# One buffer for the recurrence's output sums, and a convolution that computes in place in a buffer of its own

## The chip, the cores and the metric

The kernel runs on one core of a Trainium2 chip. The metric is the device time of one execution in microseconds. An engine is a queue that executes in the order written: TensorE (PE, with its weight loads listed as PEld), VectorE (DVE), ScalarE (ACT), GpSimd (POOL), and SyncE (SP), which here only issues transfers.

## The reference

Two layers of a mixer run over 256 context tokens and 512 latent tokens, width 2048. In each layer one input projection feeds four groups of heads, whose outputs go through one output projection. The recurrent group and the convolution group are what this change touches:

```
pl = split_proj(hl @ w_in[l]);  pc = split_proj(hc @ w_in[l])        # latent, context
yl_f, bl_f, _ = rwkv_direction(...)    # 8 heads of 64, forward; the same backward
o_C = (group_norm(y_fwd + flip(y_bwd)) + bonus_fwd + flip(bonus_bwd)) * silu(pl[10])
o_D = pl[11] * conv3(pl[12] * pl[13], conv_w) * silu(pl[14])
out = concat(o_A, o_B, o_C, o_D) @ w_out[l]
```

The second layer is the last one, and needs the outputs of the latent tokens alone.

## The kernel before

Tokens lie along the free dimension, channels on the 128 partitions. A *projection* (`proj`, `mtile`, `mstep`, L293 to L326) makes 128 channels of `h @ w_in`: weights arrive in four loads of 256 KB (`wr`), ACT casts each to a high part, POOL or DVE subtracts for the low part, and PE does 48 matmuls of 512 columns for the latent tokens and, where the context is wanted, 48 of 256 columns (L306). I count in matmuls of 512 columns, so that one of 256 is a half. The sums lie in a pool `mm` of three PSUM banks, and a bank comes free when the projection is copied or used (`evac`, `gate2`).

Each layer begins with the recurrence (`recurrence`, `rwkv_pipe`). Four pairs of heads, each with 3 segments of 256 tokens in 2 directions, make 24 *passes*, numbered 0 to 23 in each layer here; pass 6 is the first of the second pair. In a pass the state of one segment is carried through four chunks (`seg_chain`: L745, L748, L753 on PE, with small copies by DVE and ACT between them), while the matrix inverse of the next segment and the preparation of the one after it run beside it. A pass ends with its outputs (`seg_y`, L775 and L776), which are copied or added to `yacc` (L783, L785). When a pair is done, `rwkv_merge` (L863) normalises `yacc`, adds `bacc` (L884), gates, and stores it with a DMA (L888), beside the next pair's first pass.

The projections for the next pair, and after them those of the convolutions (`conv`, two in the first layer's recurrence, four in the second's), fill PE between the small matmuls. No order is written out by hand: a scheduler places every instruction by priority when the program is built, with buffers handed out in program order within a tag. A tile that shares a tag with an older one waits until the older one's last reader has finished.

The tags that matter are these, one buffer each. `x`: the `bacc` of pairs 0 and 2, and then each convolution's `x`, its first projection copied out (L1096, L1098). `o`: the `yacc` of pairs 0 and 2, and then each convolution's `o`, its running sum (L1106, L1109). `yacc` and `bacc`: those of pairs 1 and 3. A convolution's first three projections (`x`, the factor for `zp` at L1105, and the factor for L1115) need one `mm` bank each in the second layer.

Of the kernel before, what the change touches and what calls it, by code (L numbers as in the profile page):

```python
# [9 lines left out]
F32 = mybir.dt.float32  # L10
# [11 lines left out]
T = NCTX + NLAT  # L22
# [16 lines left out]
PADW = 774  # L39
# [64 lines left out]
class Kernel:  # L104
# [661 lines left out]
    def seg_y(self, s):  # L766
        l, ft, st, seg, want_y = (s[k] for k in ("l", "ft", "st", "seg", "want_y"))
        GM, SV, UV, AR = (s[k] for k in ("GM", "SV", "UV", "AR"))
        nc, rp, ps = self.nc, self.rp, self.ps
        V, A = nc.vector, nc.scalar  # L770
        if want_y:
            yp = ps.tile([128, 4, 2, 64], F32, tag="ps", name=self.nm("yp"))
            two = lambda t: t.rearrange("p a t -> p (a t)")
            for c in range(4):
                nc.tensor.matmul(out=yp[:, c], lhsT=two(UV[:, c]), rhs=GM[:, c, 1], start=True, stop=False)  # L775
                nc.tensor.matmul(out=yp[:, c], lhsT=two(SV[:, c]), rhs=AR[:, c, :, 1, :], start=False, stop=True)  # L776
            if "yacc" not in st:
                st["yacc"] = rp.tile([128, PADW], F32, tag=("o", "yacc")[ft % 2], name=self.nm("yacc"))
            ycol = st["yacc"][:, seg * SEG:(seg + 1) * SEG].rearrange("p (c t) -> p c t", c=4)
            for h in range(2):  # L780
                hs = slice(64 * h, 64 * h + 64)
                if st.get(("y", seg)):
                    V.tensor_tensor(out=ycol[hs], in0=yp[hs, :, h, :], in1=ycol[hs], op=ALU.add)  # L783
                else:
                    A.copy(out=ycol[hs], in_=yp[hs, :, h, :])  # L785
            st["y", seg] = True
# [302 lines left out]
    def conv(self, l, f):  # L1089
        nc, gp = self.nc, self.gp  # L1090
        V, G, A = nc.vector, nc.gpsimd, nc.scalar
        ctx = l < DEPTH - 1
        cs = slice(0 if ctx else NCTX, T)
        segs = ([(0, 0, NCTX, 2)] if ctx else []) + [(1, NCTX, NLAT, 260)]
        cw = self.P(l, "conv").rearrange("p (k f) -> p k f", k=3)
        x = gp.tile([128, T], F32, tag="x", name=self.nm("x"))  # L1096
        p = self.proj(l, 6336 + f * 128, ctx=ctx)
        self.evac(x[:, 0:NCTX], x[:, NCTX:T], p)  # L1098
        zp = gp.tile([128, PADW], F32, tag="stg" if gp is self.rp else "cz", bufs=2, name=self.nm("zp"))
        for c in (0, 258, 772):  # L1100
            G.memset(zp[:, c:c + 2], 0.0)
        p = self.proj(l, 6848 + f * 128, ctx=ctx)
        for i, o0, n, po in segs:
            with self.tc.high_priority():
                V.tensor_tensor(out=zp[:, po:po + n], in0=p[i][:, 0:n], in1=x[:, o0:o0 + n], op=ALU.mult)  # L1105
        o = gp.tile([128, T], F32, tag="o", name=self.nm("o"))  # L1106
        for i, o0, n, po in segs:
            s = slice(o0, o0 + n)
            A.activation(out=o[:, s], in_=zp[:, po:po + n], func=AF.Copy, scale=cw[:, 1, f:f + 1])  # L1109
            for k, d in ((0, -1), (2, 1)):  # L1110
                V.scalar_tensor_tensor(out=o[:, s], in0=zp[:, po + d:po + d + n], scalar=cw[:, k, f:f + 1],
                                       in1=o[:, s], op0=ALU.mult, op1=ALU.add)
        p = self.proj(l, 5824 + f * 128, ctx=ctx)
        for i, o0, n, po in segs:
            V.tensor_tensor(out=o[:, o0:o0 + n], in0=p[i][:, 0:n], in1=o[:, o0:o0 + n], op=ALU.mult)  # L1115
        sg = self.gate2(gp, self.proj(l, 7360 + f * 128, ctx=ctx), "stg" if gp is self.rp else "cz", 2)
        V.scalar_tensor_tensor(out=o[:, cs], in0=o[:, cs], scalar=0.5, in1=sg[:, cs], op0=ALU.mult, op1=ALU.mult)
        nc.sync.dma_start(out=self.od[12 + f][:, cs], in_=o[:, cs])
# [174 lines left out]
```

## Time and profile before

| | |
|---|---|
| three runs | 3751.83, 3750.08, 3751.13 us; median 3751.13 |
| profiled execution | 3740.13 us, of which its span 3738.3 |
| PE busy, share of the span | 3448.6 us, 92% |
| DVE, ACT, POOL busy | 2303.8, 1863.0, 1364.5 us (62%, 50%, 36%) |
| mean granted TensorE clock | 0.959 of full speed |
| first layer's recurrence, passes 0 to 23 | about 254 to 945 us |
| second layer's recurrence, passes 0 to 23 | 2313 to 2966 us |

In the rows below, busy time of an engine is the union of its instructions in a stretch; the granted clock is a share of TensorE's upper level, so that a mean of 0.68 is a mixture of its two levels, 1.0 (2.4 GHz) and 0.5 (1.2 GHz). Passes are cut at the first L745 matmul of each.

### The profile page before, as it was taken

The page shows a single profiled execution, that of the slowest core. Times are in us where ns is not written, and L with a number is a line of the kernel's source. Part 1 is how long each engine was busy: PE and PEld are TensorE (multiplying, and loading weights), DVE is VectorE, ACT ScalarE, POOL GpSimd, SP SyncE. Part 2 cuts the span into 40 slices and gives each one's busy share as a digit, 9 for nine tenths or more (in the row PEclk, how much of TensorE's full clock was granted, in tenths as well). Part 3 has the DMA queues.
Part 4 walks back from the last instruction along what each step waited for, and adds up shares of the span by engine and source line. Part 5 has one row for each costly group of instructions (what it writes and reads, how often), then busy time and mean ns, then how long its engine had stood idle before and what let it go on. Part 6 is the DMA issues. An engine that isn't in the chain of part 4 may idle for free. (4 is left out here: it accounts for less than half of the span.)

```text
span 3738.3 us, 61946 instructions
## 1 busy us (share of the span) xinstructions
PE 3448.6 (92%) x22388; PEld 2811.2 (75%) x22388; DVE 2303.8 (62%) x4659; ACT 1863.0 (50%) x4131; POOL 1364.5 (36%) x1729
## 2 busy tenths in 40 slices
PE   7999999989999999999897899999778999999998
PEld 2477777767877888888676777777566787788798
DVE  5856777777386546463878734767667526643354
ACT  4466666766244344223324435767666524544454
POOL 2244444534222222222444433545334332322343
PEclk9999999989999999999999999999668999999999
DMA  8432222211343313344655433122011244423565
GB/s 306 183 116 65 59 66 67 60 48 38 104 130 96 112 51 95 112 139 134 201 156 184 123 115 89 56 69 60 28 29 46 60 133 132 139 71 85 166 188 179
DMA packets 239747, 400.90 MB, mean 107 GB/s; under 512 B 25936, under 2 KB 95568, under 8 KB 235344
## 3 DMA queue, kind: packets, MB, share of 16 engines
q1 hardware_dynamic: 232528, 386.45, 34.3%
q10 hardware_dynamic: 6912, 10.49, 0.8%
q8 instruction: 176, 2.88, 0.3%
q14 instruction: 131, 1.07, 0.1%
HBM read 363.28 MB, written 33.56 MB: 106 GB/s over the span
## 5 line engine op out<-in xcount | busy, mean ns | idle before, releaser
L306 PE MATMUL p<-h,wh 128*128 128x512 f32 (+3 forms) x8576 | 2160.1, 349 | 34.5 <-ACT y L1160 10.7
L306 PEld LDWEIGHTS p<-h,wh 128*128 128x128 f32 (+1 forms) x8576 | 1415.4, 190 | 236.1 <-ACT h L276 15.8
L306 PE MATMUL p<-h,wl 128*128 128x512 f32 (+2 forms) x4288 | 1344.5, 350 | 46.1 <-DVE wl L277 28.9
L277 POOL TENSOR_TENSOR wl<-wr,wh 128x512 fp32r<-128x512 f32 (+1 forms) x535 | 768.4, 1439 | 1501.7 <-ACT wh L276 1317.8
L276 ACT CAST wh<-wr 128x512 fp32r<-128x512 f32 (+1 forms) x756 | 465.8, 617 | 974.1 <-PE p L306 772.2
L306 PEld LDWEIGHTS p<-h,wl 128*128 128x128 f32 (+1 forms) x4288 | 748.4, 190 | 147.7 <-DVE wl L277 35.8
L222 DVE SCALAR_TENSOR_TENSOR acc<-gw,sil,acc 128x512 f32<-128x512 f32 (+1 forms) x636 | 458.5, 778 | 27.4 <-DMA gw<-in_w_mod 25.1
L277 DVE TENSOR_TENSOR wl<-wr,wh 128x512 fp32r<-128x512 f32 (+1 forms) x221 | 160.9, 728 | 218.6 <-ACT wh L276 216.8
L804 PEld LDWEIGHTS <-ib 128*128 128x128 f16 x2304 | 133.2, 103 | 138.1 <-issue 70.0
L839 ACT CAST ib<-xa 64x256 f16<-64x256 f32 x480 | 176.2, 367 | 18.0 <-PE xa L809 12.2
L829 DVE TENSOR_TENSOR T<-inv,c 128x256 f16<-128x256 f32 x240 | 98.9, 412 | 34.5 <-PE inv L804 31.4
L1001 DVE TENSOR_REDUCE sm<-s 128x1 f32<-128x256 f32 (+1 forms) x144 | 74.8, 538 | 73.5 <-PE s L999 72.3
L741 POOL TENSOR_SCALAR sp<-SV,pcs 64x64 f32<-64x64 f32 x160 | 80.8, 509 | 105.5 <-DVE SV L762 81.0
L652 POOL TENSOR_TENSOR bk<-t_tw,kr 64x256 f32<-64x256 f32 x96 | 92.9, 968 | 36.1 <-DVE kr L636 32.4
L745 PE MATMUL ch<-SV,GM 128*128 128x128 f32 x384 | 89.5, 317 | 17.5 <-DVE SV L762 10.1
L1008 ACT ACTIVATE e<-s,sm 128x256 f32<-128x256 f32 (+1 forms) x144 | 80.9, 569 | 41.6 <-DVE sm L1005 33.3
L706 PE MATMUL g<-AR,BK 128*128 128x256 f32 (+1 forms) x384 | 96.7, 391 | 3.9 <-DVE BK L658 1.9
L748 PE MATMUL ch<-zs,xb 128*128 128x64 f32 x384 | 81.3, 296 | 15.0 <-ACT zs L747 13.6
L748 PEld LDWEIGHTS ch<-zs,xb 128*128 128x128 f32 x384 | 65.7, 204 | 38.5 <-ACT zs L747 32.5
L753 PE MATMUL ch<-UV,BKT 128*128 128x128 f32 x352 | 85.6, 328 | 9.6 <-ACT UV L750 8.6
L762 DVE SCALAR_TENSOR_TENSOR SV<-ch,pcs,sp 64x64 f32<-64x64 f32 x256 | 72.1, 281 | 35.4 <-PE ch L753 28.2
L745 PEld LDWEIGHTS ch<-SV,GM 128*128 128x128 f32 x384 | 64.4, 204 | 37.6 <-issue 9.3
(270 smaller groups left out, 5022.0 us busy)
## 6 DMA issues: line engine op xcount, KB each, us to landing
wr<-in_w_in SPq DMA_DIRECT2D x484, 256.0 KB, 2.7
wr<-in_w_out SPq DMA_DIRECT2D x256, 256.0 KB, 2.9
gw<-in_w_mod SPq DMA_DIRECT2D x192, 256.0 KB, 3.0
gw<-in_w_mod SPq DMA_DIRECT2D x32, 1024.0 KB, 6.6
gw<-in_w_mod SPq DMA_DIRECT2D x128, 128.0 KB, 3.2
raw<-rkvd SPq DMA_DIRECT2D x96, 128.5 KB, 2.2
lz<-lzd SPq DMA_DIRECT2D x48, 256.0 KB, 3.1
os<-od SPq DMA_DIRECT2D x32, 256.0 KB, 3.2
```

Source lines behind the costliest of these rows:

```text
L222: self.nc.vector.scalar_tensor_tensor(out=acc, in0=w, scalar=s, in1=acc, op0=ALU.mult, op1=ALU.add)
L276: self.nc.scalar.copy(out=hi, in_=raw)
L277: eng.tensor_tensor(out=lo, in0=raw, in1=hi, op=ALU.subtract)
L306: nc.tensor.matmul(out=p[0:w, 0:n], lhsT=a[:, kk, :], rhs=x[b][k], start=(first and kk == 0 and i == 0), stop=(last and kk == 3 and i == 2))
L652: G.tensor_tensor(out=bk[hs, :, h, :], in0=c4(an)[hs], in1=kn[hs], op=ALU.mult)
L706: nc.tensor.matmul(out=g[:, c], lhsT=bkc(c2 + c), rhs=AR[:, c2 + c, :, 0:nk, :], start=True, stop=True)
L745: nc.tensor.matmul(out=chp[:, 0:128], lhsT=two(GM[:, c, 0]), rhs=two(SV[:, c]), start=True, stop=True)
L748: nc.tensor.matmul(out=chp[:, 128:192], lhsT=XT32[:, c, :], rhs=zs, start=True, stop=True)
L753: nc.tensor.matmul(out=chp[:, 192:320], lhsT=BKT[:, c, :], rhs=two(UV[:, c]), start=True, stop=True)
L804: nc.tensor.matmul(out=out[:, c, :], lhsT=lhsT[:, c, :], rhs=rhs(c), **kw(c))
L829: V.tensor_tensor(out=T1, in0=p1, in1=bt(self.lm(d, j)), op=ALU.mult)
L839: A.copy(out=half(XT, h), in_=aXT[hs])
```

## The change

`yacc` gets one buffer under its own tag, for all four pairs: no pair's outputs go to `o` any more, and each pair's first copy waits for the store of the pair before. In the recurrence's pool the convolution's `x` moves to the tag `o`, which nothing holds after the preparation of the two decay inputs, and the convolution sums in place: `o` is the same tile as `x`, so `x` is overwritten at L1110 of the new kernel once L1106 has read it. The convolutions of the later phase keep their two tiles.

```
-                st["yacc"] = rp.tile([128, PADW], F32, tag=("o", "yacc")[ft % 2], name=self.nm("yacc"))
+                st["yacc"] = rp.tile([128, PADW], F32, tag="yacc", name=self.nm("yacc"))
...
-        x = gp.tile([128, T], F32, tag="x", name=self.nm("x"))
+        own = gp is self.rp
+        x = gp.tile([128, PADW if own else T], F32, tag="o" if own else "x", name=self.nm("x"))
...
-        o = gp.tile([128, T], F32, tag="o", name=self.nm("o"))
+        o = x if own else gp.tile([128, T], F32, tag="o", name=self.nm("o"))
```

The instructions stay the same but for names; what changes is the order that the scheduler makes. It differs on every engine from the end of pass 6 to the end of the first layer's recurrence, and from pass 8 of the second layer's recurrence to the first projections of the attention behind it; elsewhere it is the same row for row. Three places are shown.

ACT in the second layer, where the first convolution's first projection is copied out (`x`, L333). In the kernel before this stands in pass 18 (`ch_30892` is that pass's third chunk), behind the merge of pair 2 (`yacc_29403`, `gn`), and the running sum `o` right behind it:

```order
L877 ACTIVATE gn_30801<-vp_30803,eps 128x256
L882 ACTIVATE yacc_29403<-yacc_29403,par_82 128x256
L594 ACTIVATE kr_31014<-raw_31015,mu_123 128x4x64
L747 COPY zs_30893<-ch_30892 64x64
L333 COPY x_32220<-p_32221 128x512
L276 CAST hi_30881<-t_L_30779 128x256
L594 ACTIVATE t_zk_31023<-raw_31020,mu_123 128x256
L750 COPY UV_30615<-ch_30892 64x64
L1109 ACTIVATE o_32373<-zp_32295,par_82 128x512
```

In the changed kernel it stands in pass 8 (`ch_27063` is that pass's second chunk), among the inverse (`X`, `ib`, `xa`) of the next segment:

```order
L626 ACTIVATE t_L_27107<-t_L_27107 128x256
L276 CAST hi_27116<-t_sq_27113 128x256
L835 CAST X_27056<-xa_26978 128x256
L839 CAST ib_22698<-xa_26978 64x4x64
L276 CAST wh_32336<-wr_32334 128x512
L333 COPY x_32218<-p_32219 128x512
L839 CAST ib_22698<-xa_26978 64x4x64
L750 COPY UV_26955<-ch_27063 64x64
L632 ACT_TABLE_LOAD
```

The copy moved ten passes forward, ahead of the preparation of pair 2.

PE in the second layer, the last chunk of pass 13 (`ch_29048` before, `ch_29046` now), with the matmuls of the inverse (L848) and of the scores (`g`, L706) around it. Before:

```order
L706 MATMUL g_29093<-AR_22696,BK_29024 128x256 x2
L848 MATMUL inv_29067<-X_5371_29065,GM_28784 128x128
L748 MATMUL ch_29048<-zs_29049,xb_22704 128x64
L848 MATMUL inv_29067<-X_5371_29065,GM_28784 128x128 x3
L706 MATMUL g_29098<-AR_22696,BK_29024 128x256
L753 MATMUL ch_29048<-UV_28802,BKT_28446 128x128
L706 MATMUL g_29098<-AR_22696,BK_29024 128x256
L713 MATMUL bt_29103<-cst,BK_29024 128x128 x4
L745 MATMUL ch_29117<-SV_28781,GM_28784 128x128
```

Now:

```order
L306 MATMUL p_32756<-h_21042,wh_32777 128x512
L745 MATMUL ch_29046<-SV_28440,GM_28443 128x128
L306 MATMUL p_32756<-h_21043,wh_32777 128x512
L306 MATMUL p_32756<-h_21042,wl_32778 128x512
L848 MATMUL inv_29065<-X_5369_29063,GM_28782 128x128
L748 MATMUL ch_29046<-zs_29047,xb_22702 128x64
L848 MATMUL inv_29065<-X_5369_29063,GM_28782 128x128 x3
L706 MATMUL g_29096<-AR_22694,BK_29022 128x256
L753 MATMUL ch_29046<-UV_28800,BKT_28444 128x128
L706 MATMUL g_29096<-AR_22694,BK_29022 128x256
```

Where no projection stood, three matmuls of one (`p_32756`, the last projection of the second convolution) now stand around the chunk's first matmul.

ACT in the first layer, after pass 6, where the outputs of pair 1 are first copied to `yacc_4820`, while the merge still works on `yacc_2344` of pair 0. Before:

```order
L877 ACTIVATE gn_4787<-vp_4789,eps 128x256
L747 COPY zs_4855<-ch_4854 64x64
L785 COPY yacc_4820<-yp_4811 64x256 x2
L695 COPY SV_4828<-vp_4823 64x4x64
L331 COPY stg_5865<-p_5744 128x256
L696 COPY SV_4828<-vp_4823 64x4x64
L882 ACTIVATE yacc_2344<-yacc_2344,par_80 128x256
L750 COPY UV_4849<-ch_4854 64x64
```

Now:

```order
L276 CAST hi_5007<-t_sq_5004 128x256
L742 ACTIVATE sp_4951<-SV_4463,pcs_4324 64x64
L598 COPY zv_4924<-zv_4924 128x4x64
L747 COPY zs_4955<-ch_4954 64x64
L785 COPY yacc_4820<-yp_4811 64x256 x2
L714 COPY BKT_4832<-bt_4843 128x512
L750 COPY UV_4849<-ch_4954 64x64
```

The copy moved behind the second chunk's `zs` (`ch_4954`) of pass 7; the copy `BKT` stood behind it before too, and still does.

## Rows read from the trace of the kernel before

**Rows 1.** Page, 40 slices of the span: tenths of PE busy, and granted clock.

```profile
PE   7999999989999999999897899999778999999998
PEclk9999999989999999999999999999668999999999
```

**Rows 2.** Windows: stretch, length, busy PE PEld DVE ACT POOL (count), clock, DMA, GB/s.

```profile
2313.40:2586.40 273.00, 259.68 (x2186) 205.14 (x2187) 200.93 (x478) 191.86 (x486) 132.53 (x234) 0.99 0.23 65
2586.40:2844.50 258.10, 194.33 (x1476) 156.76 (x1475) 174.21 (x432) 164.48 (x418) 91.03 (x196) 0.68 0.10 28
2844.50:2963.50 119.00, 111.10 (x866) 83.35 (x866) 83.15 (x199) 74.69 (x192) 53.45 (x85) 0.99 0.19 52
2963.50:3071.00 107.50, 107.50 (x482) 88.43 (x481) 26.36 (x35) 35.55 (x57) 39.00 (x37) 1.00 0.39 112
```

**Rows 3.** Windows of line L306 alone (PE, PEld), passes 10 to 18, second layer.

```profile
2586.40:2844.50 258.10, 5.09 (x11) 2.10 (x11) 0.68 0.10 28
```

**Rows 4.** Timeline, pass 18: start, length, engine, line [idle before, releaser].

```profile
2837.95 0.72 POOL L884 TENSOR_TENSOR yacc<-yacc,bacc 128x256 f32<-128x256 f32 x1
...
2838.70 0.59 ACT L333 COPY x<-p 128x512 f32<-128x512 f32 x1 [0.75 <-POOL yacc L884]
...
2841.18 0.72 ACT L1109 ACTIVATE o<-zp,par 128x512 f32<-128x512 f32 x1 [0.23 <-DMA od<-yacc]
```

**Rows 5.** Timeline, ACT, copies of first projections behind the recurrence.

```profile
2984.93 0.58 ACT L333 COPY x<-p 128x512 f32<-128x512 f32 x1
...
3028.45 0.58 ACT L333 COPY x<-p 128x512 f32<-128x512 f32 x1
...
3071.97 0.58 ACT L333 COPY x<-p 128x512 f32<-128x512 f32 x1
```

**Rows 6.** Windows, second layer, passes 6, 8, 9, 12, 13, 21, 22.

```profile
2466.10:2502.70 36.60, 34.49 (x269) 27.49 (x268) 25.36 (x57) 25.31 (x60) 16.18 (x28) 1.00 0.21 62
2530.00:2557.30 27.30, 25.79 (x212) 19.20 (x211) 20.98 (x49) 19.14 (x49) 14.40 (x26) 1.00 0.25 69
2557.30:2586.40 29.10, 27.98 (x224) 21.28 (x223) 21.93 (x52) 22.41 (x54) 17.19 (x28) 1.00 0.26 73
2639.50:2676.50 37.00, 24.78 (x170) 18.96 (x169) 25.60 (x61) 23.14 (x57) 12.43 (x27) 0.63 0.10 30
2676.50:2700.60 24.10, 18.30 (x153) 14.18 (x151) 17.37 (x44) 18.52 (x46) 10.14 (x21) 0.72 0.11 32
2898.50:2930.50 32.00, 29.27 (x229) 22.57 (x230) 22.75 (x52) 21.09 (x51) 15.50 (x24) 1.00 0.14 38
2930.50:2951.40 20.90, 19.96 (x179) 14.85 (x178) 12.55 (x33) 10.76 (x32) 6.08 (x10) 1.00 0.14 40
```

**Rows 7.** Windows, first layer, passes 12, 18, 19.

```profile
610.10:644.60 34.50, 31.98 (x250) 25.25 (x249) 26.04 (x56) 22.72 (x56) 15.52 (x25) 1.00 0.21 60
784.20:818.20 34.00, 24.26 (x173) 17.74 (x171) 24.24 (x55) 19.72 (x50) 11.05 (x22) 0.71 0.07 21
818.20:853.70 35.50, 33.83 (x280) 29.17 (x281) 27.03 (x62) 26.25 (x62) 16.87 (x28) 0.94 0.25 72
```

**Rows 8.** Timeline, first layer: first outputs of pair 1 against pair 0's store.

```profile
471.32 0.75 ACT L785 COPY yacc<-yp 64x256 f32<-64x256 f32 x2 [0.65 <-PE yp L776]
...
475.68 0.32 SPq L888 DMA_DIRECT2D od<-yacc  x1
...
479.58 0.21 ACT L747 COPY zs<-ch 64x64 f32<-64x64 f32 x1
```

**Rows 9.** Page, DMA issues: KB each, median us to landing.

```profile
od<-yacc SPq DMA_DIRECT2D x4, 384.0 KB, 2.5
...
rot<-in_rot SPq DMA_DIRECT2D x2, 64.0 KB, 4.1
```

**Rows 10.** Timeline: last outputs of the second layer, and their merge's store.

```profile
2966.82 0.39 PE L776 MATMUL yp<-AR,SV 128*128 128x128 f32 x2
...
2984.28 0.33 SPq L888 DMA_DIRECT2D od<-yacc  x1
```

## The prediction

> **What bounds the kernel now.** I read the page's slices first: PE is busy nine tenths almost everywhere, and its granted clock is full except in slices 29 to 31 of 40, where busy drops to seven tenths and the clock to 0.6 [rows 1]. That is the second layer's recurrence. The windows cut it by its passes: 0 to 9 last 273.0 us with PE busy 259.7 at a clock of 0.99; 10 to 18 last 258.1 us with PE busy 194.3 at 0.68; then 119.0 us to the end, and 107.5 us of convolution projections with PE busy throughout [rows 2]. In passes 10 to 18 PE runs eleven projection matmuls [rows 3]: the filler is gone. Its cause is in pass 18: the first convolution's `x` is copied out of PSUM at 2838.70, right at the end of the `bacc` addition that last reads the tag `x` (2837.95 + 0.72), and `o` starts at 2841.18, released by the store of `yacc`, which held the tag `o` [rows 4]. Until then the convolution's first three projections fill the three banks of `mm`, and no projection can start.
>
> The price of filler comes from two places. Behind the recurrence the `x` copies of successive convolutions stand 43.52 us apart [rows 5], for 4 projections of 48 matmuls: 0.2267 us a matmul. In the recurrence I counted from the order 249,088 projection columns in passes 0 to 9, that is 486.5 matmuls of 512, or 110.3 us; the other 162.7 us are the passes' own. Pass 6, with a merge, has 74.5 matmuls in 36.6 us [rows 6], own time 19.7; the other nine passes average 15.9.
>
> **The change, part by part.** *Second layer, what leaves.* From the last pass's first chunk to the end of the second attention projection (`k`), the order before has 471 matmuls more than the new one (13 + 9 x 48 of convolution, 26 of `q`). Gone from there: 471 x 0.2267 = 106.8 us, all on the path, since PE is busy 107.5 of 107.5 us there [rows 2].
>
> *What arrives.* Passes 10 to 18 get 488 matmuls instead of 11. If they then behave like the filled ones they last 7 x 15.9 + 2 x 19.7 + 488 x 0.2267 = 261.3 us, against 258.1: 3.2 us lost. This is the centre of the argument: a pass without filler is no shorter than one with it. Pass 12 takes 37.0 us bare and its counterpart, pass 6, takes 36.6 filled; pass 13 is 24.1 bare, while passes 8 and 9, filled with 55 and 54 matmuls of the first convolution, take 27.3 and 29.1 [rows 6]. Passes 19 to 22 get 6 matmuls fewer: 1.4 us gained. Together 106.8 - 3.2 + 1.4 = 105.0 us.
>
> What hides the other work that moves along: the stretch behind the recurrence, with two and a half convolutions and their weight splits, has DVE, ACT and POOL busy 26, 36 and 39 us; added to 174, 164 and 91 in passes 10 to 18 that is 200, 200 and 130 of 258 [rows 2], the share that DVE has in pass 8 already (21.0 of 27.3) [rows 6]. The weight loads go into SP's queue ahead of the recurrence's own loads, and the DMA share rises from 0.10 to the 0.25 of pass 8 [rows 6]. The `zp` memsets on POOL move with them and are too short to count. If this cover fails, a pass is longer by what pass 21 shows: 32.0 us with 50 matmuls is an own time of 20.7, where its kind (pass 9: 29.1 with 54) has 16.9, so +3.8; pass 22, 20.9 with 36, has 12.7, so -3.2 against the average [rows 6]. Passes 19 to 22 together, 2844.5 to 2951.4 [rows 2, 6] with 177 matmuls, average 16.7, 0.8 above; I take 0, and 2 us a pass either way, 26 us over 13 passes, for the range.
>
> *The first layer* has the same stop, once: pass 18 has 13 matmuls in 34.0 us at a clock of 0.71 [rows 7]. The new order puts 79.5 there, 3.5 more in pass 19 and 46 more in the others: 116 that leave the stretch behind, 26.3 us. The 46 cost 10.4. Pass 18 becomes 19.6 of its own (pass 12: 34.5 less 68 x 0.2267 is 19.1; pass 6 by the same reckoning 20.0) plus 18.0, or 37.6: 3.6 lost. Pass 19, 35.5 at a clock of 0.94, becomes 33.9: 1.6 gained. Net 13.9 us.
>
> *The one `yacc`.* Pair 1's first copy ran at 471.32; pair 0's store was issued at 475.68 [rows 8] and lands 2.5 us later [rows 9], at 478.2. At its old place the copy would wait 6.9 us, with ACT's whole queue behind it, the chain's `zs` and `UV` first. At its new place it follows the second chunk's `zs`, which ran at 479.58 [rows 8]; the wait is then gone. What remains is one of two `ps` banks held some 8 us longer. There are three such changes of pair in the first layer; the second layer's first two passes of a pair give no output, so none there. I take 2 us in all; bounds 0 and 3 x 6.9 = 21.
>
> *In place.* A convolution's `x` must now wait for the store of the one before it, 2.5 us by the store of `yacc` [rows 9], but its own projection lies between (10.9 us): nothing. If that cover goes, at most 2.5 us of filler four times.
>
> *The end of the recurrence.* Convolutions used to cover the last merge, from the last outputs at 2966.82 to its store at 2984.28 [rows 10]. Now the rest of `k` does, 61 matmuls or 14 us, and the attention's tables are loaded behind that store on SP: some 17.5 us and 4.1 for `rot` [rows 9], while PE stands at its `rot` matmul after 14 us of `k`, 2 of merge and 4 of `v`. With `x` of the attention in one buffer, `v` waits once more. I take 6 us, bounds 0 and 20.
>
> *Sum.* 105.0 + 13.9 - 2 - 6 = 111 us. The profiled execution took 3740.1, so 3629; the median of the runs is 11.0 above that execution, and from it comes 3640, which I predict.
>
> A filled stretch has PE busy 95% (259.7 of 273.0) and weight loads 75% (205.1) [rows 2]. The Trainium skill, Perfetto Trace Analysis, section Identifying the Most-Contended Engine, calls matmul busy a poor measure for TensorE and takes the share of weight loads; by it a quarter of a filled pass would be free. The 49.5 matmuls a pass would then cost nothing and the sum would be some 14 us better. The trace speaks against it: a pass grows with its filler, 36.6 with 74.5 against 27.3 with 55.
>
> **The rivals.** *The chain and the filler add up (slower).* If each chunk, waiting behind filler in PE's queue, delays the next by all of it, passes 10 to 18 take 258.1 + 477 x 0.2267 = 366 us, both layers' gains vanish, and the 6 us at the end and up to 21 us of `yacc` remain: up to 3751 + 27 = 3778. It decides from a mean of 41 us a pass. For it: the bare passes have PE idle only 25% of the time. Against: passes 8 and 9.
>
> *The clock stays low (slower).* If filled passes kept the 0.68 of the bare ones, 261.3 would become 384 us: 3751 - 106.8 - 1.4 + 126 + 8 - 14 = 3763. Filled passes 8, 9, 21 and 22 all show 1.00 [rows 6], after PE had been busy 95% of its time. The Trainium skill, TensorE: Matmul & The Clock Gate, section A second HAM failure mode: psum-queue depth-cycling, describes a stream that cycles through PSUM banks and oscillates between the levels; by that rule this rival would come true, and those four windows do not bear it out.
>
> *The convolution's own work hurts.* Every one of 13 passes costs the 3.8 us of pass 21: 50 us less gain, 3690. For it: pass 21 itself, and DVE at 78%. Against: pass 22.
>
> *Nothing moves.* `x` finds another wait and the banks stay full: 3751. The order shows the copy ten passes earlier, so this needs a wait that the order doesn't show.
>
> **How the numbers follow.** Forecast 0.83, convolution's work 0.10, chain 0.03, clock 0.02, nothing 0.02. The range is the forecast's with its bounds: 26 us of pass length either way gives 3614 to 3666, the longer waits at the end and of `yacc` (14 and some of 19) stretch the upper end to 3680; I take 3616 to 3680, which leaves half of the second case and the slower ones out. A change of 0.2%, 7.5 us, is what a measurement can tell. Faster are the first two cases, 0.93; same 0.02; slower 0.05.
>
> **What would show it.** Right: passes 10 to 18 of the second layer with about 54 projection matmuls each, a clock of 0.95 or more, and 255 to 280 us in all; hardly 15 us of projections between the last outputs and the attention; pass 18 of the first layer without its idle time; no ACT wait over 2 us before L785. Wrong: a mean over 31 us in those nine passes, L785 waiting for the store with `zs` late behind it, or PE idle for over 15 us at the first attention.

## The result, and the profile after

The changed kernel takes 3644.8 us (median of four runs, 3642.8 to 3646.8), the kernel before 3750.6 (3742.5 to 3751.8). The ratio is 0.9722, with a 95% interval of 0.9705 to 0.9739: 105.8 us faster by the medians, where 111 were predicted. The profiled executions, 3646.3 and 3740.1, are 93.8 us apart; the four runs of the kernel before lie nine microseconds apart, and its profiled execution was shorter than all of them.

The page's slices of the changed kernel (PE busy and granted clock, in tenths) answer to [rows 1].

```profile
PE   6999999999999999999988899999999998999998
PEclk9999999999999999999998999999999999999999
```

The hole in slices 29 to 31 is gone, and with it the clock of 0.6. The windows of the second layer's recurrence answer to [rows 2]; the columns are the same.

```profile
2311.80:2587.40 275.60, 261.21 (x2185) 206.35 (x2186) 203.90 (x481) 193.07 (x488) 133.30 (x234) 0.99 0.22 65
2587.40:2851.30 263.90, 249.15 (x1954) 188.49 (x1953) 200.83 (x456) 189.95 (x462) 132.55 (x234) 0.99 0.24 69
2851.30:2966.00 114.70, 110.27 (x871) 81.60 (x870) 80.05 (x197) 74.11 (x195) 54.74 (x83) 1.00 0.19 54
2966.00:2984.00 18.00, 17.06 (x98) 14.26 (x97) 9.22 (x11) 7.02 (x12) 4.35 (x5) 1.00 0.18 53
```

Passes 10 to 18 are the second row: 263.9 us where they took 258.1, at a clock of 0.99 where it was 0.68. The 107.5 us of projections behind the recurrence have shrunk to part of the last row. What arrived is seen in the groups of line L306 within these nine passes, against eleven matmuls in [rows 3], and in the copies of the four convolutions' first projections, which in [rows 4, 5] began at 2838.70:

```profile
L306 PE MATMUL p<-h,wh 128*128 128x512 f32 x326 | 122.1, 426 | 0.0
L306 PE MATMUL p<-h,wl 128*128 128x512 f32 x162 | 68.8, 425 | 0.0
```

```profile
L333 ACT COPY x<-p x4: 578/583/590, 2539.4 to 2852.8; 128x512 f32<-128x512 f32 x4
```

326 and 162 make the 488 that the order gave. The first `x` is copied at 2539.4, 299 us earlier than before, the fourth at 2852.8, and no idle time stands before any of them: no wait for the in-place buffer is seen.

The first layer, against [rows 7]: the windows of pass 13, pass 18 and pass 19, and then line L785's output copies of pair 2 with what they waited for.

```profile
651.00:688.30 37.30, 33.64 (x277) 27.82 (x276) 25.98 (x57) 24.64 (x59) 15.45 (x27) 1.00 0.25 75
798.20:834.80 36.60, 34.69 (x266) 27.68 (x264) 28.99 (x63) 24.10 (x57) 16.01 (x26) 1.00 0.19 52
834.80:869.10 34.30, 32.79 (x273) 27.08 (x273) 24.79 (x57) 23.50 (x57) 16.05 (x28) 1.00 0.23 66
```

```profile
L785 ACT COPY yacc<-yp x2: 367/368/368, 661.4 to 661.8; 64x256 f32<-64x256 f32 x2
  DMA od<-yacc: 0.2, 1
```

Pass 18 is full. The one wait for the shared `yacc` is 0.2 us, in pass 13; at the other two changes of pair there is none, and VectorE's additions to `yacc` (L783) never wait for it.

The end of the second layer's recurrence, which answers to [rows 10], is where the changed kernel stands. Rows of the timeline of PE, SP, ACT and DVE from 2983, with what the engine waited for in brackets:

```profile
2983.09 0.33 SPq L888 DMA_DIRECT2D od<-yacc  x1
2984.15 0.73 PE L306 MATMUL p<-h,wh 128*128 128x512 f32 x2 [0.84 <-ACT x L333]
2985.38 1.49 SPq L898 DMA_DIRECT2D cs<-in_rope  x1
2986.91 0.43 SPq L900 DMA_DIRECT2D rot<-in_rot  x1
2990.27 0.70 PE L959 MATMUL rot<-x,rot 128*128 128x512 f32 x1 [1.73 <-DMA rot<-in_rot]
2992.86 0.69 DVE L963 TENSOR_TENSOR x<-x,rs 128x512 f32<-128x512 f32 x1 [0.73 <-POOL x L962]
2995.64 0.72 ACT L220 ACTIVATE acc<-gw,sil 128x512 f32<-128x512 f32 x1 [11.54 <-DMA gw<-in_w_mod]
2996.27 1.24 ACT L969 CAST q<-x 64x512 fp32r<-64x512 f32 x2
2998.67 0.37 ACT L331 COPY x<-p 128x256 f32<-128x256 f32 x1 [1.16 <-DVE q L971]
2999.10 0.80 PE L306 MATMUL p<-h,wh 128*128 128x256 f32 x2 [3.58 <-ACT x L331]
```

PE stands three times, 6.2 us in all: for a copy, for the table `rot`, and for `k`'s copy into the one buffer `x`, which `q` holds until ACT and DVE have worked on it. The rotated `q` is ready at 2993.55 (2992.86 + 0.69), but ACT's queue has the scaling of a modulation weight (L220) first, which waits for its load until 2995.64: `q`'s casts begin at 2996.27, 2.7 us late.

### The profile page after: what moved, and what is told of

Its sections match the earlier page's. It is cut to its first block, busy times and chain, and to the rows that moved or that the text cites. A ratio compares the mean times of both kernels' runs of the same rounds, so it can differ in the third digit from the quotient of the medians.

```text
span 3644.5 us, 61929 instructions
## 1 busy us (share of the span) xinstructions
PE 3408.4 (94%) x22388; PEld 2760.2 (76%) x22388; DVE 2314.2 (63%) x4659; ACT 1859.2 (51%) x4131; POOL 1360.0 (37%) x1729
## 5 line engine op out<-in xcount | busy, mean ns | idle before, releaser
L306 PE MATMUL p<-h,wh 128*128 128x512 f32 (+3 forms) x8576 | 2193.8, 352 | 40.4 <-ACT x L331 11.7
L306 PEld LDWEIGHTS p<-h,wh 128*128 128x128 f32 (+1 forms) x8576 | 1420.5, 191 | 240.2 <-ACT h L276 16.2
L306 PE MATMUL p<-h,wl 128*128 128x512 f32 (+2 forms) x4288 | 1356.2, 353 | 40.0 <-DVE wl L277 26.1
L306 PEld LDWEIGHTS p<-h,wl 128*128 128x128 f32 (+1 forms) x4288 | 752.7, 191 | 138.8 <-DVE wl L277 32.2
L804 PEld LDWEIGHTS <-ib 128*128 128x128 f16 x2304 | 118.9, 99 | 124.4 <-issue 67.3
L839 ACT CAST ib<-xa 64x256 f16<-64x256 f32 x480 | 175.9, 367 | 20.0 <-PE xa L809 13.9
L706 PE MATMUL g<-AR,BK 128*128 128x256 f32 (+1 forms) x384 | 92.3, 375 | 3.3 <-DVE BK L658 1.9
L835 ACT CAST X<-xa 128x256 f16<-128x256 f32 x192 | 71.3, 372 | 46.9 <-PE xa L809 44.2
L646 DVE TENSOR_TENSOR AR<-kr,Pt 64x512 f32<-64x512 f32 (+1 forms) x96 | 90.5, 943 | 2.8 <-ACT Pt L621 0.8
L748 PEld LDWEIGHTS ch<-zs,xb 128*128 128x128 f32 x384 | 60.7, 189 | 32.4 <-ACT zs L747 24.8
L634 DVE RECIPROCAL t_sq<-t_sq 128x256 f32<-128x256 f32 x48 | 84.1, 1752 | 1.5
```

Source lines behind the costliest of these rows:

```text
L306: nc.tensor.matmul(out=p[0:w, 0:n], lhsT=a[:, kk, :], rhs=x[b][k], start=(first and kk == 0 and i == 0), stop=(last and kk == 3 and i == 2))
L634: V.reciprocal(out=sq, in_=sq)
L646: V.tensor_tensor(out=AR[hs, :, h, 0:nk, :], in0=kr[hs, :, 0:nk, :], in1=Pva[hs, :, 0:nk, :], op=ALU.mult)
L706: nc.tensor.matmul(out=g[:, c], lhsT=bkc(c2 + c), rhs=AR[:, c2 + c, :, 0:nk, :], start=True, stop=True)
L804: nc.tensor.matmul(out=out[:, c, :], lhsT=lhsT[:, c, :], rhs=rhs(c), **kw(c))
L839: A.copy(out=half(XT, h), in_=aXT[hs])
```

## The experiments

**The layers apart.** In each of two kernels both edits hold in one layer (`LL` is 1 or 0), and the other layer keeps what was there before:

```
-  st["yacc"] = rp.tile(..., tag="yacc", ...)
+  st["yacc"] = rp.tile(..., tag=("o", "yacc")[ft % 2] if l != LL else "yacc", ...)
-  own = gp is self.rp
+  own = gp is self.rp and l == LL
```

The second layer alone:

> Both edits in the second layer alone; the first layer keeps the two buffers for the output sums and the convolution's x and o of before. Theory (the whole gain is second-layer filler; in the profiled pair the matching instructions of the second layer moved by 92 us): 3750.6 - 92 = 3658, passes 10 to 18 of the second layer in 255 to 270 us with a clock over 0.95. Theory on the first layer, kept: its 9 us of the profiled pair are a true gain that a chance of the output phase hid, so this kernel is 9 us above the changed one, 3654. Theory on the first layer, given back: the output phase behind it takes back what the recurrence gains, whatever the run, so this kernel is within 2 us of the changed one, 3645 to 3647.

Measured: 3653.2 against 3741.8 us, 88.6 faster, ratio 0.9757 (0.9743 to 0.9772).

The first layer alone:

> Both edits in the first layer alone; the second layer is as before. First layer kept: 3750.6 - 9 = 3742, and passes 10 to 18 of the second layer bare, 258 us at a clock of 0.6 to 0.7. First layer given back: 3749 to 3751, first attention 9 us earlier, the start of the second layer within 2 us of before. Prediction as made: 13.9 - 2, that is 3739. Waits of the output copies for the one buffer: 0.2 us in all by the changed kernel's profile, up to 21 by the prediction's bound.

Measured: 3726.1 against 3741.8, 15.6 faster, ratio 0.9956 (0.9941 to 0.9971). The windows of passes 10 to 18 of the second layer, of the kernel with that layer changed:

```profile
2599.90:2862.20 262.30, 247.73 (x1953) 187.30 (x1952) 200.30 (x456) 189.83 (x462) 132.17 (x234) 1.00 0.24 70
```

and of the kernel with the first layer changed:

```profile
2575.60:2831.30 255.70, 191.07 (x1477) 153.84 (x1476) 174.18 (x433) 164.36 (x418) 91.16 (x196) 0.69 0.10 29
```

The parts add up: 88.6 + 15.6 = 104.2. The first layer's gain is kept: in the profile of the kernel with that layer alone the first attention begins 11.5 us earlier than before and the second layer still 10.0. It seemed lost in the first pair of profiles, where the first attention began 8.1 us earlier and the second layer only 1.6. Between the two lies a stretch (first attention to the second layer's recurrence) whose order is one and the same in the kernel before, the changed kernel and the seven others here that keep the one buffer of the attention's `x`. In their ten profiles it takes 1286.2 to 1296.5 us: 1290.0 before, 1286.2 to 1295.4 in the seven whose second layer has the convolution as before, 1295.2 to 1296.5 in the three where it has the new buffers. So a few microseconds there say nothing of the first layer. Whether the new buffers cost some 4 us there, or the three were long by chance, stays open.

**One buffer, convolution as before.** Only the tag of the output sums is changed:

```
-  tag=("o", "yacc")[ft % 2]
+  tag="yacc"
```

> One buffer for the output sums of all head pairs, but the convolution as before (x in the tag x, o in the tag o). Theory (each convolution needs both tags free; x still waits for the bacc of pair 2): no gain, 3747 to 3755; the second layer's passes 10 to 18 stay bare, and in the first layer the stop moves one pass ahead (pass 17 half empty, 18 bare), 0 to 4 us lost. Rival (the tag o, held by the output sums, was the stop that counted): passes 10 to 18 of the second layer fill, and over 50 us are gained, 3700 or less. Rival (the one buffer is dear): 3765 to 3772, the copies of the output sums waiting 7 us at each of three changes of pair.

Measured: 3756.6 against 3741.8, 14.9 slower, ratio 1.0040 (1.0026 to 1.0055). The theory had a loss of 0 to 4 us. The last rival had the size, 14 to 21 us, but not the cause: the copies wait 0.2 us for the one buffer in this profile too. The second layer's passes 10 to 18 stayed bare, as the theory said; the loss is in the first layer, whose attention starts 15 us late. Passes 17 and 18 are left with 25 and no matmuls there, as the theory also had it, but passes 7 to 15 take more of the convolution (39 matmuls by the order) and 277.0 us in place of 264.7. The windows of line L306 alone in passes 16 to 18 (length, busy PE, PEld, clock, DMA; the count is of matmuls of either width), here:

```profile
745.10:832.60 87.50, 19.56 (x66) 10.75 (x66) 0.81 0.11 31
```

in the kernel before:

```profile
732.70:818.20 85.50, 32.46 (x117) 18.47 (x117) 0.89 0.14 38
```

and in the kernel with the first layer changed:

```profile
744.50:831.40 86.90, 52.43 (x217) 33.77 (x217) 1.00 0.19 55
```

With 66, 117 and 217 matmuls (58.5, 96.5 and 163 of 512 columns) the three passes take 87.5, 85.5 and 86.9 us, at clocks of 0.81, 0.89 and 1.00. Filler taken out of a pass gives no time back, while passes 7 to 15, which are full already, are 12 us longer with 39 matmuls more: this is the prediction's centre, seen from its other side.

**Filler that does nothing.** Why is a bare pass no shorter? Four kernels add dummy matmuls, whose results nothing reads, to passes 10 to 18 of the second layer of the kernel before. The first three write unused columns of the chain's own PSUM tile, in the first two like this, with ten or four of them:

```
+  fill = lambda: [nc.tensor.matmul(out=chp[:, 320:512], lhsT=self.eyef,
+                                   rhs=self.c16[:, 0, 0:3, :], start=True, stop=True)
+                  for _ in range(10 if l == 1 and 10 <= s["n"] <= 18 else 0)]
   nc.tensor.matmul(out=chp[:, 0:128], ...)
+  fill()
```

and so behind the chain's other two matmuls of a chunk. With ten:

> The kernel before, with 30 matmuls of 192 fp16 columns that nothing reads added to each chunk of the chain in passes 10 to 18 of the second layer, ten behind each of its three matmuls (1080 in all, 0.08 us of columns each at the full clock, 86 us of PE in all). They feed no buffer and need none. Theory (the bare pass is bound by the round trips of the chain through DVE and ACT, and filler lies in their gaps while the clock rises): the nine passes still take 250 to 270 us, the clock 0.9 or more, the time within 10 us of before. Rival, clock (a bare pass is long only because its own matmuls run at 0.68): the nine passes drop by the 44 us that their own 194 us of PE are above the 150 us that filled passes need, to 215 to 225, the time to about 3710. Rival, sum (filler is added to the chain): 86 us or more longer, 3837.

Measured: 3778.9 against 3741.8, 37.1 slower, ratio 1.0093 (1.0078 to 1.0108). With four in place of ten:

> The kernel before with 12 dummy matmuls to each chunk of passes 10 to 18 of the second layer, four behind each matmul of the chain in place of ten (432 in all; by the 0.107 us that one took, 46 us of PE). The ten cost 36 us in nine passes for 116 us of PE. Theory (a block of ten holds PE 1.07 us, longer than the chain's copy takes, so each chunk waits for the end of it; short pieces of filler fit in the gaps): 255 to 263 us for the nine passes, at a clock above that of before (0.68). Rival, share (31% of filler is always paid): 258 + 14 = 272. Rival, clock: with the clock back and little filler, the passes become shorter than bare ones, under 250.

Measured: 3766.3 in one run. With ten, at low priority:

> The same 1080 dummy matmuls as in the kernel with ten behind each chain matmul (36 us longer in the nine passes), but emitted at low priority, so that the scheduler puts them where it sees PE without other work: 39 blocks of ten are left where there were 76, and 36 single ones where there were 3; most are in pieces of one to nine. Theory, place (a piece of filler costs what it holds up behind it; the convolution's projections, placed by the scheduler one or two at a time, cost 6 us for 111): 262 to 280 us for passes 10 to 18 in place of 294, the clock 0.9 or more, the time 3745 to 3763 by the medians of before. Rival, dose (a fixed share of PE work is paid, whatever its place): 290 to 298 us, 3778. Rival, the convolution's projections are hidden because they need no wait on ch: this kernel no better than the other, 294 or more.

Measured: 3814.9 against 3745.8, 69.0 slower, ratio 1.0188 (1.0158 to 1.0217). The nine passes of the three, in this order, each from its own profile:

```profile
2588.20:2882.10 293.90, 235.87 (x2520) 204.70 (x2519) 178.02 (x433) 161.50 (x415) 90.12 (x197) 0.97 0.09 26
```

```profile
2591.10:2870.30 279.20, 225.89 (x1895) 185.07 (x1894) 175.79 (x430) 163.77 (x418) 91.03 (x196) 0.76 0.09 26
```

```profile
2593.60:2925.20 331.60, 255.07 (x2581) 209.75 (x2580) 185.47 (x444) 172.19 (x431) 95.65 (x201) 0.94 0.08 23
```

All my expectations of length were wrong, but for the third rival of the last one, and the design was at fault. The groups of DVE show its copy of `UV` in the nine passes and what it waited for, in the kernel before and in the first of these:

```profile
L749 DVE COPY UV<-ch 64x64 f32<-64x64 f32 x36 | 7.5, 209 | 10.5 <-PE ch L748 10.3
...
L754 DVE COPY UV<-ch 64x64 f32<-64x64 f32 x36 | 7.8, 216 | 31.9 <-PE ch L738 30.7 <-ACT gn L880 0.9
```

L738 is the dummies' line in the second row, L748 the chain's own matmul in the first. The copy reads columns that the dummies don't touch, but they write the same tile, and it waits for their end, 30.7 us where it had waited 10.3 for the chain. DVE's other readers of the tile wait for L738 too, in all three kernels. The dummies were a part of the chain, and these kernels measure a longer chain, not filler. The fourth kernel gives them a bank of `mm` that nothing else uses:

```
+  if s["n"] == 10 and n == 0:
+      self.fill = self.mm.tile([128, 512], F32, tag="mm", ...)
+  with self.tc.high_priority(offset=-1000):
+      for _ in range(13):
+          nc.tensor.matmul(out=self.fill, lhsT=self.eyef, rhs=self.c16[:, 0, 0:8, :], ...)
```

> The kernel before with 468 dummy matmuls of 512 fp16 columns (as long as a projection matmul), at low priority, into a bank of mm that nothing else uses or reads in the second layer's passes 10 to 18; in the two kernels with dummies in the chain's own tile ch, the profile showed DVE's copies waiting for the dummies, so that these lay on the chain. Here nothing waits for them, and they bring no work for DVE, ACT or the queues. By the order 362 come to stand in passes 10 to 17, 104 in passes 5 to 9 in place of 115 matmuls of the convolution, which has two banks in place of three; 64 convolution matmuls more come behind the recurrence, 14.5 us. Theory (filler that nothing waits for lies in the gaps of PE): passes 10 to 17 take 218 to 232 us (221.3 bare, 225.8 in the changed kernel), the clock there 0.9 or more, the time 3746 + 15 = 3755 to 3770. Rival, share (a third of any filler is paid, as with the dummies of ch): 221 + 27 = 248. Rival, sum: 221 + 82 = 303. Rival, clock (bare passes are long only because of 0.68; with the clock back and no other work they are shorter): under 212.

Measured: 3733.8 against 3743.4, ratio 0.9968 (0.9956 to 0.9981): 468 matmuls that compute nothing make the kernel before faster, though 64 of the convolution's are left over at the end. Passes 10 to 17 in its profile, whole, and the dummies' line alone:

```profile
2580.10:2783.40 203.30, 194.04 (x1664) 127.32 (x1663) 149.52 (x372) 141.86 (x363) 78.92 (x174) 0.99 0.11 33
...
2580.10:2783.40 203.30, 102.16 (x362) 31.35 (x362) 0.99 0.11 33
```

the same eight passes of the kernel before:

```profile
2586.40:2807.70 221.30, 169.84 (x1308) 137.88 (x1307) 147.97 (x372) 140.53 (x360) 78.71 (x171) 0.67 0.10 28
```

and of the changed kernel, whole and line L306 alone:

```profile
2587.40:2813.10 225.70, 214.02 (x1706) 161.97 (x1705) 173.53 (x394) 163.31 (x399) 113.66 (x201) 0.99 0.24 69
...
2587.40:2813.10 225.70, 130.96 (x408) 69.92 (x408) 0.99 0.24 69
```

This is the case that I had called the clock's rival: 203.3 us, under its 212. DVE no longer waits for a dummy anywhere. Successive dummies start 0.21 to 0.23 us apart, so the 362 hold PE for some 79 us, and the eight passes are 18 us shorter than bare ones: 97 us in all.

The rows say where these 97 us come from, by estimate. PE's time without work falls from 51.5 us (221.3 less 169.8) to 9.3 (203.3 less 194.0): 42 us of the dummies lie in gaps. Its busy time rises by 24 us for 79 us of dummies: its own matmuls take 55 us less, some 115 in place of 170, as the granted clock goes from 0.67 to 0.99. In the changed kernel the gaps fall to 11.7 us, and 408 matmuls at 0.2267 us are 92.5 of the 214.0, so that PE's own work takes some 122: 40 us of gaps and 48 us of clock stand against 92.5 us of filler. So the theory of the gaps and the rival of the clock are each about half of it: a bare pass has gaps that filler can use, and it runs PE's own matmuls slowly for want of filler. What a bare pass would take at the full clock was not measured, so how much of the gaps would go by the clock alone stays open.

**The end of the recurrence.** The changed kernel again, as the base:

> The changed kernel once more, unaltered, as the base for the two that build on it and to see whether its first layer's gain is given back. Kept (the first-layer kernel kept its 13 us to the end): in this profile the first attention starts 8 to 12 us earlier than in the profile of before, and the second layer's recurrence 5 to 15 us earlier, the output phase between the layers varying by 5 us or more from run to run at one and the same order. Given back: it starts within 3 us of before, as in the first profile.

Measured: 3641.6 against 3744.4, ratio 0.9717 (0.9696 to 0.9738). The first attention starts 8.9 us earlier than in the profile of before, as "kept" had it, the second layer's recurrence 3.3 earlier, short of its 5 to 15; the stretch between, with its spread, is the one described above. Then two buffers for the attention's `x`, and what shares its tag:

```
-  x = tT("x")
+  x = tT("x", 2)
```

> The changed kernel with two buffers for the attention's x (and what shares its tag), so that k can be copied out of PSUM before q is worked up. Theory (the end of the recurrence was priced at 6 us and cost some 12 because k's copy waits for q's, which waits for the tables): PE's 3.6 us without work at 2999 in the changed kernel's profile go, and the like waits of four later attentions (2.4, 1.5, 2.4, 2.1, 3.0 us) go in part: 3 to 12 us faster than the changed kernel. Rival (the banks fill again one projection later, and v waits instead; what bounds the entrance is q's work on DVE and ACT): within 2 us of it, PE without work for the same time in the next place.

Measured: 3629.1 against 3744.4, ratio 0.9686 (0.9667 to 0.9705), 12.5 us below the base by the medians: the theory's gain, a little above its range. PE's list of waits between 1000 and 3500 us (what waited, for what: us in all, times, longest) has in the changed kernel

```profile
PE p L306 <- DVE wl L277: 21.7, 14, 3.7
...
PE p L306 <- ACT x L331: 11.7, 5, 3.6
...
PE s L997 <- ACT e L1008: 4.7, 1, 4.7
...
PE tp L942 <- ACT x L331: 4.3, 4, 2.1
```

and with two buffers

```profile
PE p L306 <- DVE wl L277: 29.6, 19, 4.0
...
PE s L997 <- ACT e L1008: 7.8, 5, 3.1
...
PE tp L942 <- ACT x L331: 0.6, 1, 0.6
```

Of 16.0 us for the copies into `x`, 0.6 are left, and 11.0 come back as waits for weight splits and exponentials. From the start of the second layer's last pass to the first `rot` matmul of its second attention (L959) this kernel takes 120.7 us; the changed kernel took 124.9 and 125.5 in its two profiles, the kernel with the second layer alone 122.8. So 2 to 5 us at the end of the recurrence hung on the one buffer. More lies elsewhere: the second layer's recurrence already starts 7.3 us earlier than in the profile of the base. With the table `rot` loaded first and the first modulation job an attention later:

```
+  self.rot = ...; nc.sync.dma_start(out=self.rot, ...)    # ahead of self.cs
-  mod_jobs(1)
+  if h or l == 0:
+      mod_jobs(1)
```

> The kernel with two buffers for x, and besides: the small table rot loaded ahead of cs, and in the second layer the first job on the modulation weights (whose first scaling on ACT waits 2.1 us for its load, with q's copies queued behind it) started one attention later. Theory: PE's 1.7 us at its rot matmul go down to under 0.5, and q's copies follow at once: 3 to 6 us faster than the kernel with two buffers alone, 6 to 15 faster than the changed one. Rival (the table cs bounds, which DVE needs right behind rot, and it lands no earlier): within 2 us of the kernel with two buffers.

Measured: 3627.3, ratio 0.9685 (0.9666 to 0.9705): no different from two buffers alone, so the rival holds. PE still waits 1.3 us for `rot`, after 1.4. DVE's first use of `cs` (L962 here) is released by the landing of `cs`, 37.8 us behind the start of the last pass, after 38.5:

```profile
2983.58 0.69 DVE L962 TENSOR_TENSOR rs<-rot,cs 128x512 f32<-128x512 f32 x1 [7.37 <-DMA cs<-in_rope]
```

`q`'s casts follow it at once, so the scaling is out of their way and nothing is gained by it. What that scaling costs with one buffer, where `k`'s copy stands behind `q`'s, was not run.

## Why the prediction was right, and where it was off

*The middle of it* was right. The order's 488 matmuls came, and the nine passes took 263.9 us (262.3 with that layer alone) for a predicted 261.3, at 0.99. "The chain and the filler add up" (366 us), "the clock stays low" (384) and "nothing moves" are refuted; "the convolution's own work hurts", which had 3.8 us more a pass, found 2.6 us more in all nine. The section of the Trainium skill on which the clock's rival leaned (TensorE: Matmul & The Clock Gate, section A second HAM failure mode: psum-queue depth-cycling) ties its oscillation to short idle times of PE between groups of matmuls; a stretch that goes through three banks with PE busy 94% stays at 0.99 here. That a pass without filler is no shorter was read from the rows rightly, but without its cause. The dummies show it, by the estimate above: PE's gaps, and the clock, each worth about half of the filler. One of the readings was weak: that "a pass grows with its filler, 36.6 with 74.5 against 27.3 with 55", for the first of the two passes has a merge, 3.8 us of own time by the prediction's own count.

*The term that was mis-sized is the end of the recurrence*, taken at 6 us. Against 106.8 us of matmuls that left, the second layer behind the start of its last pass gained 95.1 (the profiles' gain of 93.8 at the end, and 1.3 lost at that pass): the term is 11.7, inside its bounds (9.9 and 12.9 by two other profiles with the same order there). All of it is lost in the first two attentions: at the third one's first `rot` matmul the gain is 94.3 already. The waits above are 6.2 of it; the kernel before has none there. The granted clock of 0.93 at 2984 to 3010, where PE is busy 20.5 us, is 1.4 more by estimate, and in the 30 us behind that PE is busy 24.95 where the kernel before had 27.30, another 2.4; 1.7 are not placed. I had counted the table's landing, and one more turn of the one buffer at `v`. What I missed is that `k`'s copy stands behind `q`'s whole work-up, 3.6 us of waiting for PE; two buffers take that wait away and give 2 to 5 us back. That the modulation weight's scaling in ACT's queue makes up to 2.7 of the 3.6 is read from the timeline, not shown by a run.

*The first layer*, 13.9 less 2, is 15.6 by the runs (11 to 22) and 11.5 at the first attention by the profile. The kernel with that layer alone shows its parts: 26.3 us leave, as the order had it (its last pass starts 14.8 us later than before, its first attention 11.5 earlier); the passes lose 16.5 where I had 12.4, and 7.2 of that in pass 13 (38.2 against 31.0), for 12 more matmuls by the order, 2.7 us. The kernel with the one buffer alone has that long pass too (37.3), the one with the second layer alone hasn't (31.0); whether the buffer or the order that comes with it makes it was not told apart. Waits for the one buffer, 2 us with a bound of 21, were 0.2.

*Smaller terms.* Passes 19 to 22 gained 5.5 us for a predicted 1.4 (106.9 to 101.4), and passes 0 to 9, left out of the sum, lost 2.6 (273.0 to 275.6). No wait for the in-place buffer was seen. The share of weight loads, by which (beside the share of peak arithmetic) the Trainium skill, Perfetto Trace Analysis, section Identifying the Most-Contended Engine, judges TensorE, would have put the sum 14 us better, away from what was measured; in the filled passes PE's busy time (94%), not that of its weight loads (188.5 of 263.9 us), is nearly full. The 49.5 matmuls a pass of that paragraph are 48.7 by its own count (486.5 in ten passes); nothing else rests on them.

*The base, and luck.* The 11 us between profile and median were not a constant of the kernel: its median was 3741.8 to 3750.6 in five measurements. The gain by medians, 103 to 106 us, is what the sum of 111 must be held against: 5 to 8 us too much. That 3640 came so near to 3644.8 and 3641.6 is in part luck, since from a base of 3742 the same sum gives 3631. And the sum is nearer than its parts: by layers it was 99.0 and 11.9, the runs gave 88.6 (85 to 96) and 15.6 (11 to 22). The second layer was over-forecast by some 10 us, of which the end of the recurrence is 5.7; the first layer came out 4 better, within its interval.

## What to carry to other kernels

Before filler is moved, compare passes with and without it, their granted clock and PE's idle time: here a thin stretch with a quarter of PE idle and a clock of 0.68 took 477 matmuls more for 4 to 6 us, and what released their first buffer decided whether they could go there. Filler must hang on nothing that the chain waits for; in the chain's own tile it becomes a part of the chain. And when a cover is taken away from a change of phase, follow each buffer and queue there up to the second projection, not only the transfer that comes first.

## What the runs showed of the hardware

- 468 matmuls whose results nothing reads made a kernel 0.32% faster (0.19 to 0.44): in eight passes PE had 79 us more to do and needed 18 us less, at a granted clock of 0.99 in place of 0.67.
- The granted clock of the nine passes was 0.68 bare, 0.76 with 432 dummies of 192 columns, 0.97 with 1080 of them in blocks of ten, and 0.94 with 1080 at low priority.
- Copies by DVE out of a PSUM tile waited for matmuls that wrote other columns of the same tile: 30.7 us in nine passes for the copy of `UV`, which had waited 10.3 us for the chain before; with a tile of the dummies' own DVE waited for none of them.
- One and the same order, of 6755 matmuls from the first attention to the second layer's recurrence, took 1286.2 to 1296.5 us in ten profiles. From 1850 to 1900 the granted clock was 0.97 in the profile of before, 0.85 and 0.83 in the two of the changed kernel.
